# A hybrid encoder layer: a prologue with whole token tiles, and other SBUF places

## The chip, the cores and the metric

The kernel runs on one core of one Trainium2 chip. The metric is the device time of one execution in microseconds; the time before is the median of three runs, 915.5 us (914.26 to 915.56). All inputs lie in the chip's memory at the start, and the output is written there.

## The reference, cut to what matters

One layer of a hybrid trunk, on 512 tokens of width 1024, in float32:

```
h  = rms_norm(x, gain)                        # per token: x * rsqrt(mean(x^2)) * gain
xa, ga, q, k, v, f, gA, gB = split(h @ w_in)  # one projection, 1024 -> 7696 columns
A  = gelu(ga) * rg_lru(causal_conv4(xa))      # recurrent branch, width 1280
B  = forgetting_attention(q, k, v, f)         # 16 heads of 64, causal
m  = sigmoid(gA) * (A @ P_A) + sigmoid(gB) * (B @ P_B)
x  = x + rms_norm(m @ w_out, gain)
h  = rms_norm(x, gain)
u  = causal_conv3(h @ w_up)                   # 1024 -> 6144
x  = x + rms_norm((gelu(u_gate) * u_val) @ w_down, gain)
```

The change concerns how the first normalisation is fed, where some weights lie in SBUF while gA, gB and w_up are multiplied, and when one block of P_B is made ready.

## The kernel before, in words

**Numbers in two parts.** Every operand of a large product is split into a high part, rounded to the format float32r (fp32r in the rows), and a low part, the rest. A product is then three products of parts: high by high, high by low, low by high (mm3, L216; project_half, L226). ScalarE makes the high part (Split.hi, L171, a copy), and VectorE, or GpSimd where lo(pool) is written, the low one (Split.lo, L174, a subtraction). In the rows wh and wl are the parts of weights, hh and hl those of the normalised input (channels on the partitions, tokens along the row, 8 blocks of 128 channels), h2h and h2l those of the second normalised input.

**Stages.** The weights come in units of 128x1024 in the order of the list `order` (L186). fetch (L201) issues a unit's load on the SP queue and its two splits; unit (L210) runs ahead by one or two units. TensorE goes through: four tiles of xa in the prologue (`half`, L623), the other xa, v, ga, the projection P_A, then q0 and k0; the merge gates (`period`, L443); attention over eight pairs of heads with q, k of the next pair (L1072 on); P_B (pb_part, L1056); w_out; w_up (`period` again, after first products at L1244 to L1290); w_down.

**The order of work.** A planner of the framework orders the instructions of each engine, but for the stretches in manual_schedule (L563, L913, L1283, L1352), where they stand as written. `tc.issue_after(i)` keeps the instructions of its block behind i on i's engine. Each engine works its own list in order.

**The prologue (L557 to L691).** GpSimd builds an identity matrix. ScalarE's queue loads one row of gains (`gone`), which TensorE spreads over 128 partitions by a product with a row of ones into two banks (pgain, L588). SP loads token tiles 0 and 1 in two halves of 512 columns each (L570), then the units xa0 and xa1, tiles 2 and 3, xa2 and xa3. For a tile, `sumsq` (L594) squares and sums each half on ScalarE, VectorE adds the two sums, and rstd_of gives the factor (a square root on ScalarE, a reciprocal on VectorE); `sumsq_whole` (L603, tiles 2 and 3) does it in one instruction of 1024 columns. `scaled(t, g)` multiplies half g by the factor and the gains on VectorE, `turn(t, g)` transposes its four blocks on TensorE, and evac_hi and evac_lo write them to hh (ScalarE) and hl (VectorE). `spin(n)` is n products of the identity with itself into a bank that is used later; they compute nothing. The written order is at L626 to L669: tile 0's first half, tile 1's sums, the rounding of unit xa0, then halves of both tiles in turns, then `half(0, X)`: unit xa0 by the first 256 tokens, that is, tiles 0 and 1.

**Gates and up loop.** Both take pairs of output blocks by seven products instead of eight (class Pair, L339). The products are numbered: 1 and 2 multiply plain weights (mh0, ml0, from the pool called stpools[0]) by a quarter of the input; 3 multiplies mh1, ml1 (stpools[1]) by a sum of quarters; 5, 6 and 7 multiply sums of weights (th, tl, in the pool of all weights) by sums of quarters (sh, sl); 4 multiplies th, tl by a plain quarter. In the gates the names carry a g in front: gmh, gml, gth, gtl, gsh, gsl. A pair's stretch runs 5, 6, 4 of the pair before, 3, then 1 and 2 of the next and 7. Each product is 12 products of 256 columns on TensorE (L418, L419, L421).

**Places.** Pools are stacked from the left and the right side of SBUF. `offset(stack, n)` puts n unused bytes (per partition) between two pools. In the kernel before, hh starts at byte 69120, gmh0 at 180160 and 184256 (two buffers), the weights' buffers for gth at multiples of 4096 from 35328, gsh0 at 196544; in the up loop h2h starts at 196544, mh0 at 126464 and 130560, up0's first weights at 85504.

**P_B.** pb_part(e, ks) takes unit pb`e` and, running one ahead, issues the load and splits of the next. pb0, pb1 and pb2 are multiplied in the attention's tail, pb3 to pb7 after it (L1129 to L1131).

Of the kernel before, what the change touches and what calls it, by code (L numbers as in the profile page):

```python
# [8 lines left out]
F32 = mybir.dt.float32  # L9
F32R = mybir.dt.float32r  # L10
BF16 = mybir.dt.bfloat16
AF = mybir.ActivationFunctionType
# [4 lines left out]
P = 128  # L17
# [46 lines left out]
def kernel(  # L64
# [421 lines left out]
    with ExitStack() as rg:  # L486
        rt, ixt, tt = {}, {}, {}
        last_act = [None]
        with ExitStack() as r0:
# [68 lines left out]
            with tc.tile_pool(name="pre", bufs=2, side="right", reuse_waits="tile") as pre, ExitStack() as wp:  # L558
# [3 lines left out]
                man = ExitStack()  # L562
                man.enter_context(tc.manual_schedule())  # L563
                warm = small.tile([P, 1], F32, name="warm", bufs=1)
                gone = pre.tile([1, D + P], F32, name="gone", bufs=1)
                pool.memset(gone[:, D:], 1.0)
                act.dma_start(gone[:, :D], gains[0:1, :])
                act.activation(out=warm, in_=epst, func=AF.Sqrt)
                xts = [pre.tile([P, D], F32, tag="xt", name=f"xt{t}", bufs=NT) for t in range(NT)]
                for t in range(2):  # L570
                    for c in HALVES:
                        nc.sync.dma_start(xts[t][:, c], xv[:, t, c])
                us = [Split(*order[t][1:], order[t][0], wpre) for t in range(2)]
                for t in range(2, NT):
                    nc.sync.dma_start(xts[t], xv[:, t])
# [10 lines left out]

                spin(4)
                pgain = [bank(f"gain{i}") for i in range(2)]  # L588
                for i in range(2):
                    pe.matmul(pgain[i], gone[:, D:], gone[:, 512 * i : 512 * i + 512], start=True, stop=True)  # L590

                xns, rss, ptr, lasts = {}, {}, {}, [None, None]

                def sumsq(t):  # L594
                    xns[t] = pre.tile([P, D], F32, tag="xn", name=f"xn{t}")
                    s2 = small.tile([P, 2], F32, tag="s2", name=f"s2_p{t}")
                    for i, c in enumerate(HALVES):
                        act.activation(out=xns[t][:, c], in_=xts[t][:, c], func=AF.Square, accum_out=s2[:, i : i + 1])
                    ss = small.tile([P, 1], F32, tag="ss", name=f"ss_p{t}")
                    dve.tensor_tensor(out=ss, in0=s2[:, 0:1], in1=s2[:, 1:2], op=ALU.add)  # L600
                    rss[t] = rstd_of(ss, f"p{t}")

                def sumsq_whole(t):  # L603
                    xns[t] = pre.tile([P, D], F32, tag="xn", name=f"xn{t}")
# [18 lines left out]
                def half(i, c):  # L623
                    project_half(pss[i], us[i].parts(), hh, hl, c)

                sumsq(0)  # L626
                scaled(0, 0)
                sumsq(1)
                us[0].hi()
                us[0].lo(pool)  # L630
                scaled(1, 0)
                turn(0, 0)
                spin(3)
                turn(1, 0)
                scaled(0, 1)
                turn(0, 1)
                evac_hi(0, 0)
                evac_lo(0, 0)
                scaled(1, 1)
                turn(1, 1)  # L640
                evac_hi(1, 0)
                evac_lo(1, 0)
                evac_hi(0, 1)
                evac_lo(0, 1)
                evac_hi(1, 1)
                evac_lo(1, 1)
                half(0, X)
                us[1].hi()
                us[1].lo(pool)
                sumsq_whole(2)  # L650
# [256 lines left out]
    with ExitStack() as g2:  # L907
        spool = g2.enter_context(tc.tile_pool(name="gsums", bufs=1, side="right", reuse_waits="tile"))
        gates.sh = [spool.tile([P, KH, SH], F32R, name=f"gsh{i}") for i in range(4)]
        gates.sl = [spool.tile([P, KH, SH], F32R, name=f"gsl{i}") for i in range(4)]  # L910
        gp[1] = Pair(gates, 1, GP[1])
        man = g2.enter_context(ExitStack())
        man.enter_context(tc.manual_schedule())  # L913
        for i, f in enumerate((fq[3], fq[0], fq[2], fq[1])):
            act.copy(gates.sh[i], f)
            sub(gates.sl[i], f, gates.sh[i].bitcast(F32))
        hfstk.close()
        st0pool = splitstk.enter_context(tc.tile_pool(name="gsplit0", bufs=2, side="right", reuse_waits="tile"))
        offset(splitstk, 448, "right")
        st1pool = splitstk.enter_context(tc.tile_pool(name="gsplit1", bufs=2, side="right", reuse_waits="tile"))  # L920
        gates.stpools = [st0pool, st1pool]
        none = Nothing()
        p, n = gp[0], gp[1]
        p.plain_high(0)
        p.plain_high(1)
        p.p12()
        p.p5()
        n.sums(0)
        n.sums(1)
        n.plain_low(0)  # L930
        n.plain_high(0)
        n.sums_hi(0)
        n.sums_hi(1)
        p.keep(2, p.a[:, Y])
        p.add(p.a[:, X], p.a[:, X], 2)
        p.keep(1, p.c[:, X])
        n.sums_lo(0)
        n.sums_lo(1)
        gp[2] = Pair(gates, 2, GP[2])

        def more(j):
            if j + 3 < len(GP):
# [12 lines left out]
        bias = prep_alloc(0)  # L955
        b = gp.pop(len(GP) - 1)
        b.add(b.c[:, Y], b.a[:, Y], 1)
        b.add(b.c[:, X], b.c[:, X], 0)
        gate_epilogue(b, "c", 0)
        fetch(where["k1"])  # L960
        gate_epilogue(b, "c", 1)

    with ExitStack() as at:
# [47 lines left out]
        def pt(p, pts):  # L1011
# [10 lines left out]
            for j in range(2):  # L1022
# [4 lines left out]
                for i0, i1, src, o in ((0, 8, tbs[j], 0), (8, 10, rest, P * j)):  # L1027
                    for half in range(2):
                        ps = src[half][:, o : o + (i1 - i0) * HD].rearrange("p (i c) -> p i c", c=HD)
                        act.copy(thv[:, i0:i1, half], ps)  # L1030
                        dve.tensor_tensor(out=tlv[:, i0:i1, half], in0=ps, in1=thv[:, i0:i1, half].bitcast(F32), op=ALU.subtract)
                res.append((th, tl))
            return res
# [22 lines left out]
        def pb_part(e, ks):  # L1056
            if e not in pb:
                pb[e] = bank(f"pb{e}")
                pbw[e] = unit(f"pb{e}", 1)
            wh, wl = pbw[e]  # L1060
            for k in ks:
                mm3(pb[e], wh[:, k], wl[:, k], yb[k][:, 0], yb[k][:, 1], k == 0, k == KD - 1)

        rounded = []

        def behind(name, ahead=2):
            with tc.issue_after(rounded[-1].ins):
# [70 lines left out]
    mstk.close()  # L1138

    fstk = ctx.enter_context(ExitStack())  # L1140
    offset(fstk, 96)
    xpool = fstk.enter_context(tc.tile_pool(name="x2", bufs=1, reuse_waits="tile"))
    x2t = xpool.tile([P, NT, D], F32, name="x2t")
    nc.sync.dma_start(x2t, xv)
# [14 lines left out]

    turned = {}  # L1160
    with ExitStack() as mix:
        wfpool = mix.enter_context(tc.tile_pool(name="wfirst", bufs=2, reuse_waits="tile"))
        npool = mix.enter_context(tc.tile_pool(name="norm", bufs=2, reuse_waits="tile"))
        special["up0"] = special[f"up{JF}"] = wfpool
        hf = npool.tile([P, KD, S], F32, name="hf", bufs=1)
        gb = [npool.tile([P, D], F32, name=f"gain{i}", bufs=1) for i in range(2)]
        nstk = ExitStack()
# [115 lines left out]
        with tc.manual_schedule():  # L1283
# [8 lines left out]
            p.sums_lo(0)  # L1292
            next(s3, None)

    ypool = fstk.enter_context(tc.tile_pool(name="ff", bufs=3, reuse_waits="tile"))
    ydram = ctx.enter_context(tc.tile_pool(name="ffd", bufs=1, space=bass.MemoryType.DRAM))
    yd = [ydram.tile([P, 2, S], F32, name=f"yd{j}") for j in range(JF // 2)]
# [427 lines left out]
```

## Time and profile before

| | us |
|---|---|
| median of three runs | 915.5 |
| lowest and highest | 914.26, 915.56 |
| the profiled execution | 915.62 |
| its span, from first to last instruction | 913.8 |

The profile is that of one execution. PE is TensorE's products, PEld its weight loads, DVE VectorE, ACT ScalarE, POOL GpSimd, and SPq the SP queue's issue of transfers. A row of the timeline has the start, the length, the engine, the line, the operation, out<-in by names, the shape and the count, and in brackets the idle time before it with what ended it. Products overlap in the pipeline, so a product's own length is longer than its distance to the next; where many follow each other, the time of a whole stretch divided by their count is the pace. A row of a stretch (start:end) has the length, then the busy time of each engine with its count of instructions, the clock, and the load of the DMA engines. A row of a group has the count, and behind the bar the busy time and the mean length in ns.

### The profile page before, as it was taken

The numbers are of one execution on the slowest core, as the hardware profiler recorded it, in microseconds if no ns is written. First come the engines' busy times: TensorE is split into PE (matmuls) and PEld (weight loads), VectorE is DVE, ScalarE is ACT, GpSimd is POOL, SyncE is SP. The second block draws the span as 40 slices with busy tenths as digits, with TensorE's granted clock in tenths as the row PEclk, the third lists the DMA queues.
The fourth block names the chain that finished last, engine by engine and source line by source line (L and its number), as shares of the span: only waits on it lengthen the run. The fifth ranks groups of instructions, "written<-read, shape, count | busy, mean of one in ns | idle before, by whom it ended". The sixth has DMA issues, their size and how long they took to land.

```text
span 913.8 us, 15945 instructions
## 1 busy us (share of the span) xinstructions
PE 904.4 (99%) x5906; PEld 805.5 (88%) x5906; DVE 726.0 (79%) x1197; ACT 601.6 (66%) x1041; POOL 218.9 (24%) x281
## 2 busy tenths in 40 slices
PE   8999999999999999999999999999999999999997
PEld 7988888887899998888888889999999999988886
DVE  4966359737777649888878588989999999889897
ACT  6565496423377757677654477878888888677664
POOL 4134444534111112212104200132323223100000
PEclk9999999999999999999999999999999999999999
DMA  7677669989968767435424654468988888699764
GB/s 261 234 214 207 191 166 274 256 229 182 212 164 198 199 222 261 180 128 174 139 93 156 208 180 160 116 174 201 231 227 209 236 210 211 205 397 328 243 200 148
DMA packets 72048, 187.86 MB, mean 206 GB/s; under 512 B 7265, under 2 KB 27793, under 8 KB 71586
## 3 DMA queue, kind: packets, MB, share of 16 engines
q1 hardware_dynamic: 47648, 127.72, 41.9%
q0 software_dynamic: 24176, 58.99, 29.8%
q8 instruction: 46, 0.75, 0.3%
q14 instruction: 32, 0.26, 0.1%
q10 hardware_dynamic: 146, 0.14, 0.0%
HBM read 150.69 MB, written 35.73 MB: 204 GB/s over the span
## 4 chain that ended last, share of the span: by engine, by line
PE 96%; DVE 1%; DMA 1%; ACT 1%; SPq 0%; issue 0%; DVEq 0%; ACTq 0%
PE up L421 7%; PE up L419 7%; PE up L418 7%; PE dn L1434 4%; PE dn L1432 4%; PE dn L1433 4%; PE pa L217 2%; PE ga L218 2%; PE ga L217 2%; PE pa L219 2%; PE pa L218 2%; PE ga L219 2%; PE k L217 2%; PE q L217 2%; PE wo L1151 2%; PE pb L217 2%
## 5 line engine op out<-in xcount | busy, mean ns | idle before, releaser
L1309 DVE SCALAR_TENSOR_TENSOR u<-up,cpt,u 128x511 f32<-128x511 f32 x96 | 71.3, 746 | 3.5 <-ACT u L1303 1.8
L362 POOL DMA_DIRECT2D ml<-raw_up x41 | 35.3, 861 | 152.6 <-ACT ml L361 89.5
L1434 PE MATMUL dn<-wh_dn,al 128*128 128x512 f32 (+1 forms) x180 | 67.7, 376 | 0.0
L1433 PE MATMUL dn<-wl_dn,ah 128*128 128x512 f32 (+1 forms) x180 | 67.5, 375 | 0.0
L1432 PE MATMUL dn<-wh_dn,ah 128*128 128x512 f32 (+1 forms) x180 | 67.5, 375 | 0.0
L419 PE MATMUL up<-sl,th 128*128 128x256 f32 x252 | 60.2, 276 | 0.0
L418 PE MATMUL up<-sh,th 128*128 128x256 f32 x252 | 60.2, 276 | 0.0
L175 DVE TENSOR_TENSOR wl_dn<-raw_dn,wh_dn 128x1024 fp32r<-128x1024 f32 x42 | 51.3, 1222 | 9.3 <-ACT wh_dn L172 9.2
L172 ACT CAST wh_dn<-raw_dn 128x1024 fp32r<-128x1024 f32 x42 | 44.1, 1050 | 21.2 <-PE dn L1434 7.3
L1303 ACT ACTIVATE u<-up,cpt 128x512 f32<-128x512 f32 x48 | 36.9, 778 | 21.6 <-PE up L421 11.6
L324 DVE TENSOR_TENSOR tl<-t,th 128x1024 fp32r<-128x1024 f32 x42 | 51.0, 1217 | 0.0
L419 PEld LDWEIGHTS up<-sl,th 128*128 128x128 f32 x252 | 47.3, 188 | 0.0
L418 PEld LDWEIGHTS up<-sh,th 128*128 128x128 f32 x252 | 47.3, 188 | 0.0
L1317 POOL TENSOR_TENSOR yf<-u,u 128x512 f32<-128x512 f32 x23 | 31.4, 1365 | 63.3 <-issue 48.8
L400 ACT CAST th<-t 128x1024 fp32r<-128x1024 f32 x42 | 43.8, 1045 | 3.3 <-DVE t L324 0.8
L418 PE MATMUL up<-h2h,mh 128*128 128x256 f32 x168 | 40.2, 276 | 0.0
L419 PE MATMUL up<-h2l,mh 128*128 128x256 f32 x168 | 40.2, 276 | 0.0
L1434 PEld LDWEIGHTS dn<-wh_dn,al 128*128 128x128 f32 x180 | 33.9, 188 | 6.8 <-DVE al L324 0.7
L1433 PEld LDWEIGHTS dn<-wl_dn,ah 128*128 128x128 f32 x180 | 33.9, 188 | 6.1
L1432 PEld LDWEIGHTS dn<-wh_dn,ah 128*128 128x128 f32 x180 | 33.9, 188 | 6.0
L421 PE MATMUL up<-sh,tl 128*128 128x256 f32 x252 | 38.8, 276 | 0.0
L998 ACT ACTIVATE P<-P,mx 128x384 f32<-128x384 f32 (+3 forms) x64 | 35.2, 553 | 4.2 <-DVE mx L993 3.3
(717 smaller groups left out, 3239.1 us busy)
## 6 DMA issues: line engine op xcount, KB each, us to landing
raw_up<-in_w_up_dram SPq DMA_DIRECT2D x48, 512.0 KB, 5.4
td<-in_w_down_dram POOLq DMA_DIRECT2D x36, 512.0 KB, 6.0
raw_dn<-td SPq DMA_DIRECT2D x24, 512.0 KB, 5.2
B<-cnd POOLq DMA_DIRECT2D x16, 640.0 KB, 5.5
ml<-raw_up POOLq DMA_DIRECT2D x20, 512.0 KB, 5.8
raw_dn<-in_w_down_dram SPq DMA_DIRECT2D x18, 512.0 KB, 4.3
raw_wo<-in_w_out_dram SPq DMA_DIRECT2D x16, 512.0 KB, 3.9
td<-td POOLq DMA_DIRECT2D x12, 512.0 KB, 10.6
```

The costliest lines, as they stand in the source:

```text
L172: act.copy(self.wh, self.raw)
L175: engine.tensor_tensor(out=self.wl, in0=self.raw, in1=self.wh.bitcast(F32), op=ALU.subtract)
L217: pe.matmul(dst, ah, bh, start=first, stop=False)
L324: dve.tensor_tensor(out=out, in0=a, in1=b, op=ALU.subtract)
L400: act.copy(self.th[i], self.t[i])
L418: pe.matmul(dst, wh[:, k], ah[:, k], start=first and k == 0, stop=False, skip_group_check=True)
L419: pe.matmul(dst, wh[:, k], al[:, k], start=False, stop=False, skip_group_check=True)
L421: pe.matmul(dst, wl[:, k], ah[:, k], start=False, stop=k == KH - 1, skip_group_check=True)
L1309: dve.scalar_tensor_tensor(out=c[:, s:], in0=ps[:, : S - s], scalar=col(C_CFW + 3 * e + j), in1=c[:, s:], op0=ALU.mult, op1=ALU.add)
L1432: pe.matmul(d[:, x], ah[:, k, tok], wh[:, k, x], start=first, stop=False, skip_group_check=True)
L1433: pe.matmul(d[:, x], ah[:, k, tok], wl[:, k, x], start=False, stop=False, skip_group_check=True)
L1434: pe.matmul(d[:, x], al[:, k, tok], wh[:, k, x], start=False, stop=last, skip_group_check=True)
```

## The change

- Tiles 0 and 1 are loaded by one transfer each, and squared whole (`sumsq_whole`); `sumsq` goes.
- The gains' row is split into a high and a low part on VectorE (four instructions of one partition and 512 columns), and four products of float32r replace the two of float32. The row of ones and the parts lie in buffers of the pool xc; the tile `gone` is 512 bytes shorter.
- Two fillers are added ahead of tile 0's transposes.
- The order of the prologue: both halves of tile 0 are scaled and transposed, then the three fillers, then tile 1's sums, the rounding of unit xa0, tile 0's two high parts; tile 1 is scaled and transposed by halves; the low parts come behind.
- The first stretch of xa0 takes all eight products high by high, then the eight with hl, then the eight with wl, where it took high by high and high by low in turns.
- The 448 bytes between the gates' two weight pools become 384 ahead of the first and 64 between them: the first (gmh0, gml0) moves by 384 bytes, the second stays.
- The 96 bytes ahead of the residual x2t go behind it; the pool of the first up weights is parted in two with 96 bytes between, so that up0's weights move by 96 bytes and up24's stay. What comes later keeps its place.
- In attention's tail the unit fetched ahead by pb_part(2), which is pb3, is held behind the last copy of pair 6's transposed probabilities on ScalarE.

```
-                gone = pre.tile([1, D + P], F32, name="gone", bufs=1)
-                pool.memset(gone[:, D:], 1.0)
-                act.dma_start(gone[:, :D], gains[0:1, :])
+                gone = pre.tile([1, D], F32, name="gone", bufs=1)
+                act.dma_start(gone, gains[0:1, :])
...
                 for t in range(2):
-                    for c in HALVES:
-                        nc.sync.dma_start(xts[t][:, c], xv[:, t, c])
+                    nc.sync.dma_start(xts[t], xv[:, t])
...
-                for i in range(2):
-                    pe.matmul(pgain[i], gone[:, D:], gone[:, 512 * i : 512 * i + 512], start=True, stop=True)
+                one = xpool.tile([P, S], F32R, tag="xc", name="one")[0:1, :P]
+                pool.memset(one.bitcast(F32), 1.0)
+                for i, c in enumerate(HALVES):
+                    gh, gl = (xpool.tile([P, S], F32R, tag=x, name=f"gain_{x}{i}")[0:1] for x in ("xh", "xl"))
+                    dve.tensor_copy(out=gh, in_=gone[:, c])
+                    dve.tensor_tensor(out=gl, in0=gone[:, c], in1=gh.bitcast(F32), op=ALU.subtract)
+                    for j, g in enumerate((gh, gl)):
+                        pe.matmul(pgain[i], one, g, start=j == 0, stop=j == 1)
...
-                sumsq(0)
+                spin(2)
+                sumsq_whole(0)
                 scaled(0, 0)
-                sumsq(1)
+                scaled(0, 1)
+                turn(0, 0)
+                turn(0, 1)
+                spin(3)
+                sumsq_whole(1)
                 us[0].hi()
                 us[0].lo(pool)
-                scaled(1, 0)
-                turn(0, 0)
-                spin(3)
-                turn(1, 0)
-                scaled(0, 1)
-                turn(0, 1)
                 evac_hi(0, 0)
-                evac_lo(0, 0)
-                scaled(1, 1)
-                turn(1, 1)
-                evac_hi(1, 0)
-                evac_lo(1, 0)
                 evac_hi(0, 1)
-                evac_lo(0, 1)
-                evac_hi(1, 1)
-                evac_lo(1, 1)
-                half(0, X)
+                for g in range(2):
+                    scaled(1, g)
+                    turn(1, g)
+                for g in range(2):
+                    evac_lo(0, g)
+                for g in range(2):
+                    evac_hi(1, g)
+                    evac_lo(1, g)
+                wh, wl = us[0].parts()
+                for w, h in ((wh, hh), (wh, hl), (wl, hh)):
+                    for k in range(KD):
+                        pe.matmul(pss[0][:, X], w[:, k], h[:, k, X], start=w is wh and h is hh and k == 0, stop=w is wl and k == KD - 1)
...
+        offset(splitstk, 384, "right")
         st0pool = splitstk.enter_context(tc.tile_pool(name="gsplit0", bufs=2, side="right", reuse_waits="tile"))
-        offset(splitstk, 448, "right")
+        offset(splitstk, 64, "right")
...
-                        act.copy(thv[:, i0:i1, half], ps)
+                        copied[p] = act.copy(thv[:, i0:i1, half], ps)
...
-                pbw[e] = unit(f"pb{e}", 1)
+                with ExitStack() as held_back:
+                    if e == 2:
+                        held_back.enter_context(tc.issue_after(copied[KD - 2].ins))
+                    pbw[e] = unit(f"pb{e}", 1)
...
-    offset(fstk, 96)
     xpool = fstk.enter_context(tc.tile_pool(name="x2", bufs=1, reuse_waits="tile"))
...
-        wfpool = mix.enter_context(tc.tile_pool(name="wfirst", bufs=2, reuse_waits="tile"))
+        wfpools = [mix.enter_context(tc.tile_pool(name="wfirst0", bufs=1, reuse_waits="tile"))]
+        offset(mix, 96)
+        wfpools.append(mix.enter_context(tc.tile_pool(name="wfirst1", bufs=1, reuse_waits="tile")))
...
-        special["up0"] = special[f"up{JF}"] = wfpool
+        special["up0"], special[f"up{JF}"] = wfpools
...
+    offset(fstk, 96)
     ypool = fstk.enter_context(tc.tile_pool(name="ff", bufs=3, reuse_waits="tile"))
```

More of the change, by code (lines that the diff above doesn't have):

```diff
@@ L588 @@
                 pgain = [bank(f"gain{i}") for i in range(2)]
-                for i in range(2):
-                    pe.matmul(pgain[i], gone[:, D:], gone[:, 512 * i : 512 * i + 512], start=True, stop=True)
-                xns, rss, ptr, lasts = {}, {}, {}, [None, None]
[L594 to L601, printed above, removed]
+                one = xpool.tile([P, S], F32R, tag="xc", name="one")[0:1, :P]
[6 more added lines that the diff above has]
+                        pe.matmul(pgain[i], one, g, start=j == 0, stop=j == 1)
+                xns, rss, ptr, lasts = {}, {}, {}, [None, None]
                 def sumsq_whole(t):
@@ L1062, in pb_part @@
                 mm3(pb[e], wh[:, k], wl[:, k], yb[k][:, 0], yb[k][:, 1], k == 0, k == KD - 1)
-        rounded = []
+        rounded, copied = [], {}
         def behind(name, ahead=2):
```

## The prediction

> **What bounds the kernel now.** The first page of the profile comes first, for the span, the load of each engine and the chain that ended last.
>
> ```profile
> span 913.8 us, 15945 instructions
> PE 904.4 (99%) x5906; PEld 805.5 (88%) x5906; DVE 726.0 (79%) x1197; ACT 601.6 (66%) x1041; POOL 218.9 (24%) x281
> PE 96%; DVE 1%; DMA 1%; ACT 1%; SPq 0%; issue 0%; DVEq 0%; ACTq 0%
> ```
>
> TensorE works 99% of the span, and 96% of the chain is TensorE. So I asked the view of waits what TensorE waited for in the whole span, and it has two rows:
>
> ```profile
> PE xa L585 <- POOL ident masks.py:199: 1.5, 1, 1.5
> PE tr_p L245 <- DVE xn L611: 1.2, 1, 1.2
> ```
>
> Both lie in the first 11 us. So three things can shorten this kernel: an earlier start of the products (now 13.65), an earlier end of TensorE's slow pace, and a shorter time per product in the 900 us behind. The timeline of the front:
>
> ```profile
> 0.74 2.19 SPq L572 DMA_DIRECT2D xt<-in_x_dram  x4
> 1.49 2.08 PE L585 MATMUL xa<-ident 128*128 128x128 f32 x8 [1.49 <-POOL ident masks.py:199]
> 2.98 0.91 SPq L166 DMA_DIRECT2D raw_xa<-in_w_in_dram  x2
> 3.50 3.78 PE L590 MATMUL gain<-gone 1*128 1x512 f32 x4
> 3.84 0.63 ACT L598 ACTIVATE xn<-xt 128x512 f32<-128x512 f32 x1 [1.03 <-DMA xt<-in_x_dram]
> 4.47 0.63 ACT L598 ACTIVATE xn<-xt 128x512 f32<-128x512 f32 x1
> 6.02 0.75 DVE L611 SCALAR_TENSOR_TENSOR xn<-xt,rs_p,gain 128x512 f32<-128x512 f32 x1
> 7.21 1.12 PE L245 MATMUL tr_p<-ident,xn 128*128 128x128 f32 x4
> 8.11 1.49 PE L585 MATMUL xa<-ident 128*128 128x128 f32 x6
> 8.54 0.63 ACT L598 ACTIVATE xn<-xt 128x512 f32<-128x512 f32 x1 [2.21 <-DMA xt<-in_x_dram]
> 9.92 1.04 ACT L172 CAST wh_xa<-raw_xa 128x1024 fp32r<-128x1024 f32 x1
> 10.82 3.18 PE L245 MATMUL tr_p<-ident,xn 128*128 128x128 f32 x12 [1.22 <-DVE xn L611]
> 10.87 0.58 ACT L249 CAST hh<-tr_p 128x512 fp32r<-128x512 f32 x1
> 13.65 0.56 PE L229 MATMUL xa<-hh,wh_xa 128*128 128x256 f32 x1
> 15.65 2.42 POOL L175 TENSOR_TENSOR wl_xa<-raw_xa,wh_xa 128x1024 fp32r<-128x1024 f32 x1 [2.20 <-ACT wh_xa L172]
> 16.14 0.41 PE L230 MATMUL xa<-hl,wh_xa 128*128 128x256 f32 x1
> 16.35 0.41 PE L229 MATMUL xa<-hh,wh_xa 128*128 128x256 f32 x1
> 16.78 0.29 PE L229 MATMUL xa<-hh,wh_xa 128*128 128x256 f32 x1
> ```
>
> and, from the chain in order of time (start, length, what):
>
> ```profile
> 20.02 0.94 PE xa L232 x8
> ```
>
> The reader is to see four things. Tile 1's second half lands at 8.54. The first weights land at 9.9, and their rounding on ScalarE holds up tile 0's evacuation, which was ready. VectorE's last scaling stands behind an evacuation, so the last transposes come late. And the first products are 0.21 us apart (16.14 to 16.35), later ones 0.12 (eight in 0.94): TensorE runs at about half pace until 16.7.
>
> **The front.** (1) Issue: SP spends 2.19 us on four half tiles, and 0.91 on two transfers of a whole 512 KB. Two whole tiles cost about 0.9, so all behind them is issued 1.3 us sooner, and the first weights land at about 9.9 - 1.3 = 8.6.
>
> (2) Tile 0 lands between 3.84 (its first half) and 4.47, where ScalarE took the second half; I take 4.3. A whole tile's way to its scaling is shown by tile 2:
>
> ```profile
> 15.46 1.06 ACT L606 ACTIVATE xn<-xt 128x1024 f32<-128x1024 f32 x1
> 17.17 1.41 DVE L611 SCALAR_TENSOR_TENSOR xn<-xt,rs_p,gain 128x512 f32<-128x512 f32 x2
> ```
>
> That is 1.71 us to the start and 3.12 to the end of both halves. Tile 0 is scaled from 6.0 to 7.4, its first half no later than now (6.02). The add of two half sums goes.
>
> (3) The gain rows: two full fp32 products took four passes of 0.94 us (3.78). Four rounded ones replace them. A rounded product of 256 columns takes 0.21 at half pace, so one of 512 about 0.42: 1.7 us. They need two copies and two subtractions of 1x512 on VectorE, at most 0.7 each by the 0.75 of the 128x512 scaling: 2.8 us from 3.5 at worst, done at 6.3 beside tile 0's squaring. Covered; without the cover scaling would start 0.3 late. The two fillers (a third of 1.49 each, 1.0 together) run while tile 0 is scaled.
>
> (4) TensorE then has tile 0's eight transposes (four take 0.9, from 7.21 to 8.11), three fillers (1.4) and tile 1's eight, all in its own order: 6.75 + 1.8 + 1.4 = 9.95, and + 1.8 = 11.7. Tile 1 must be scaled by then. Its landing is not shown for a whole tile. The rate by half-microseconds gives the early bound:
>
> ```profile
> GB/s 0 0 0 41 291 340 365 250 201 254 176 303 369 336 369 381 389 418 393 401 401 451 426 393 418 410 409 400 392 398 338 360 384 168 86 49 25 8 123 131
> ```
>
> Summed, 1.05 MB (both tiles) are in by 5.8; the late bound is today's 8.54. I take 7.0: scaled from 8.7 to 10.1, in time for 9.95 and 10.8. ScalarE rounds the weights from 8.6 to 9.7 and evacuates tile 0 by 10.7, before tile 1 needs it. The lower halves on VectorE run beside the first eight products, which no longer need them: the new order takes all eight upper by upper products first. So the first product starts at about 11.7 instead of 13.65: **1.95 us**. Bounds: with the landing at 8.54 the scaling ends at 11.66, + 0.9 is 12.6, and with the clock opening no earlier half of the 1.05 us is lost: 0.6. At best, below.
>
> (5) The clock. The page's clock line shows no step in the front, so I go by the distance of products. From 1.49 to 9.6 TensorE was hardly idle, with fillers, gain rows and transposes, and stayed at half pace; it sped up 3.05 us after real products began. I take the same distance again, so the start's 1.95 us is kept whole. Were the opening fixed at 16.7, the extra time would be worth 0.12/0.21 of it: 1.1. Were it opened by the denser fillers before 11.7, the 3.05 us at half pace (worth 1.3) would go too, and transposes would shorten: up to 3.9.
>
> [...]
>
> What follows is fed in time: POOL's low part of the second weights ends at 18.07 and is first used at 20.02, the eight products above; its cause, ScalarE's rounding behind the last evacuation, moves forward with the evacuation.
>
> **SBUF places.** They move no work, yet products of one shape differ by operands:
>
> ```profile
> L418 PE MATMUL mb<-gsh,gth 128*128 128x256 f32 x48 | 11.8, 281 | 0.0
> L418 PE MATMUL mb<-hh,gmh 128*128 128x256 f32 x32 | 7.7, 276 | 0.0
> L418 PE MATMUL mb<-hh,gth 128*128 128x256 f32 x16 | 4.0, 282 | 0.0
> L418 PE MATMUL up<-sh,th 128*128 128x256 f32 x252 | 60.2, 276 | 0.0
> 280.63:284.87 4.24, 4.24 (x39) 4.24 (x37) 3.02 (x7) 2.86 (x6) 0.86 (x1) 1.00 0.97 280
> 600.47:604.54 4.07, 4.07 (x38) 4.07 (x37) 2.61 (x5) 3.15 (x7) 2.67 (x3) 1.00 0.17 65
> ```
>
> The last two are 36 products each (7, 5 and 6) of a gates pair and of an up pair: 4.24 against 4.07 us. By the allocator's addresses in the kernel before, the moving tile's place less the weights', modulo 512, is 448 in both; but in the gates the products ahead (hh by gmh) stand at 64, while in the up loop they stand at 448 as well. So the pace seems to be lost at the switch from 64 to 448. The 384 bytes put gmh0 and gml0 at 448 from hh, like the rest. If the pace then holds, 0.17 us times eight pairs is 1.4; I keep **1.1 us**, since the first pair or two enter from another state than the rest. Bounds: nothing, 1.4, or, if hh by gmh went to the 282 of hh by gth, 192 x 6 ns = 1.2 us lost. I take the row of the up loop, whose places are the same.
>
> The up loop's first products show the same two paces, 48 products each:
>
> ```profile
> 555.70:561.35 5.65, 5.65 (x49) 5.65 (x48) 5.65 (x11) 3.69 (x10) 0.00 (x0) 1.00 0.72 220
> 579.83:585.26 5.43, 5.43 (x50) 5.43 (x49) 5.40 (x8) 5.26 (x8) 0.87 (x1) 1.00 0.56 180
> ```
>
> The 96 bytes now stand between up0's weights and up24's; up0's move alone. That can end the slow pace after up0: 0.3 us at most, and up0's second half may slow by 0.1. I take **0.2**. The residual's move touches no product.
>
> **The held-back unit.** The last fetch before the tail puts pb3's rounding here:
>
> ```profile
> 453.51 1.05 ACT L172 CAST wh_pb<-raw_pb 128x1024 fp32r<-128x1024 f32 x1 [2.47 <-PE k L218]
> 454.47 0.57 ACT L970 CAST h_k<-k 128x512 fp32r<-128x512 f32 x1
> 455.74 0.68 DVE L971 TENSOR_TENSOR l_k<-k,h_k 128x512 fp32r<-128x512 f32 x1
> 467.09 0.46 ACT L1030 CAST PTh<-pt_r 128x128 fp32r<-128x128 f32 x2 [1.31 <-DVE PTl L1031]
> 469.25 0.58 ACT L1048 COPY ytmp<-av 64x512 f32<-64x512 f32 x1 [1.70 <-PE av L1045]
> ```
>
> It stands ahead of k7's upper half, which the last scores need. The new wait puts it behind the copies that end at 467.55; ScalarE has 1.70 us free there, and 1.05 fit. Queued behind it on ScalarE is the copy ytmp, for which VectorE's sum y and then the last unit's attention output wait; the copy loses nothing as long as the 1.70 hold. VectorE's low part follows the rounding, and pb3 is multiplied only behind the whole tail (L1131). The gain is at most the 1.05 by which k7's half came late, and the view of waits has no row of TensorE for it, so it is near nothing: **0.1**. The loss is at most 1.05, if the copy waited for the whole rounding.
>
> **Sum.** 1.95 + 1.1 + 0.2 + 0.1 = 3.35 us. The profiled execution took 915.62 us (span 913.8 and 1.8 around it), 0.1 above the median of 915.5. 915.62 - 3.35 = **912.3 us**.
>
> **The rivals.** *The clock opens at the same moment*: for it, the 8 us at half pace; against it, nothing fixes 16.7. The front gives 1.1: 913.1. [...] *The fillers open it early*: for it, TensorE is unbroken from 6.75; against it, the same 8 us. The front gives 1.95 + 1.0 (half to all of the 1.3): 911.3. *Tile 1 lands where it does now and the places do nothing*: for it, the 2.21 us wait for a half of tile 1, and no run shows gmh at its new place. Only the 0.6 of the front stays: 915.0, no change. *Slower*: the up loop falls into the slow pace as the gates have it. A pair's 36 products would cost 0.17 us more, and by the same 5 ns its 24 of products 1 and 2 0.12; the 252 of the row above, 12 a pair, make 21 pairs: 21 x 0.29 = 6.1, and 915.62 - 3.35 + 6.1 = 918.4. It passes the time before from the twelfth slow pair on. For it: its first 96 products are slow today, and the places there change; against it: today the last tile's transposes, among those first products, end that.
>
> **How the numbers follow.** 0.40 for the forecast, 0.22 for the same moment, 0.15 for the early clock, 0.14 for no change, 0.09 for slower. The range 910.2 to 915.3 reaches from the early clock with its upper bound to the case without change; it leaves out the slow up loop and a little at the fast end. A difference of 0.2% (1.8 us) is about what a measurement of this kernel can tell from none: under 913.8 is faster. The first three cases are faster but for a few parts in a hundred: 0.76; the same 0.15; slower 0.09.
>
> **What would show it.** Right: the first L229-like product near 11.7, the distance of products falling to 0.12 near 14.8 (11.7 + 3.05), the gates' gsh by gth at 276, wh_pb behind 467. Wrong: tile 1's squaring starting at 8.5, gsh by gth still at 281, or up products at 281.

## The result, and the profile after

| | before | changed | ratio, 95% interval |
|---|---|---|---|
| median of 22 runs each | 914.54 us (913.03 to 916.43) | 913.12 us (912.10 to 914.45) | 0.9983 (0.9977 to 0.9989) |
| profiled execution | 915.62 us, span 913.8 | 912.16 us, span 910.4 | |

By the medians the change gains 1.4 us (1.0 to 2.1 by the interval), 0.17%: under the prediction's bound of 0.2%, so "the same" by that bound, though the interval excludes zero. The two profiled executions differ by 3.5 us. That overstates it: the profile of before lies 1.1 above its median, the profile of after at the fast end of its kernel. A comparison of just these two traces would have confirmed the forecast of 3.35.

The page of after, for the span and the load:

```profile
span 910.4 us, 15950 instructions
PE 901.1 (99%) x5910; PEld 804.1 (88%) x5910; DVE 727.8 (80%) x1199; ACT 601.6 (66%) x1037; POOL 220.2 (24%) x281
```

The timeline of its front (start, length, what, idle before it):

```profile
0.75 0.87 SPq L570 DMA_DIRECT2D xt<-in_x_dram  x2
4.51 1.06 ACT L601 ACTIVATE xn<-xt 128x1024 f32<-128x1024 f32 x1 [1.70 <-DMA xt<-in_x_dram]
4.95 0.62 PE L594 MATMUL gain<-gain_xl,one 1*128 1x512 f32 x1
5.50 1.22 PE L583 MATMUL xa<-ident 128*128 128x128 f32 x4
7.18 1.94 PE L245 MATMUL tr_p<-ident,xn 128*128 128x128 f32 x8 [0.46 <-DVE xn L606]
7.25 1.03 ACT L172 CAST wh_xa<-raw_xa 128x1024 fp32r<-128x1024 f32 x1
8.91 0.89 PE L583 MATMUL xa<-ident 128*128 128x128 f32 x6
9.64 1.04 PE L245 MATMUL tr_p<-ident,xn 128*128 128x128 f32 x8
10.91 1.23 PE L644 MATMUL xa<-hh,wh_xa 128*128 128x256 f32 x8 [0.24 <-ACT hh L249]
11.98 1.10 PE L644 MATMUL xa<-hl,wh_xa 128*128 128x256 f32 x8
```

Look at the two rows of fillers: four passes take 1.22 us at 5.50, six take 0.89 at 8.91. Tile 0's eight transposes take 1.94, tile 1's 1.04. TensorE came to full pace at about 9, before the first product. The trace's record of the granted clock, which the views do not print, has it open at 9.03, against 16.79 in the profile of before. The first product starts at 10.91 instead of 13.65, and the first half unit ends 4.1 us earlier.

In the gates, the groups of products of their stretch (count, busy us, mean ns of one, idle before), and in a second fence the held-back rounding from ScalarE's timeline:

```profile
L418 PE MATMUL ma<-gsh,gth 128*128 128x256 f32 x48 | 11.6, 278 | 0.0
L418 PE MATMUL mb<-gsh,gth 128*128 128x256 f32 x48 | 11.5, 277 | 0.0
L418 PE MATMUL mb<-hh,gmh 128*128 128x256 f32 x32 | 7.9, 281 | 0.0
L421 PE MATMUL mb<-hh,gml 128*128 128x256 f32 x32 | 5.1, 281 | 0.0
```

```profile
463.52 1.05 ACT L172 CAST wh_pb<-raw_pb 128x1024 fp32r<-128x1024 f32 x1
```

The 281 of gsh by gth went to 277 (276 was predicted). But hh by gmh, 276 before, now takes the 281: the slow pace has moved to another product. The rounding stands at 463.5; with the 3.84 us by which all of that stage is earlier this is 467.4 in the time of before, where the prediction looked for it.

The waits of TensorE in the whole span:

```profile
PE xa L583 <- POOL ident masks.py:199: 1.5, 1, 1.5
PE tr_p L245 <- DVE xn L606: 0.5, 1, 0.5
PE tr_f L260 <- DVE xn L1197: 0.4, 1, 0.4
PE xa L644 <- ACT hh L249: 0.2, 1, 0.2
```

The third is new and lies at 561 us: part of the gain is given back there, ahead of the last norm's transposes.

### The profile page after: what moved, and what is told of

Same layout as the page of the kernel before. It is cut to its first block, busy times and chain, and to the rows that moved or that the text cites. A ratio compares the mean times of both kernels' runs of the same rounds, so it can differ in the third digit from the quotient of the medians.

```text
span 910.4 us, 15950 instructions
## 1 busy us (share of the span) xinstructions
PE 901.1 (99%) x5910; PEld 804.1 (88%) x5910; DVE 727.8 (80%) x1199; ACT 601.6 (66%) x1037; POOL 220.2 (24%) x281
## 4 chain that ended last, share of the span: by engine, by line
PE 97%; DVE 1%; ACT 1%; DMA 0%; issue 0%; DVEq 0%; ACTq 0%
PE up L421 7%; PE up L418 7%; PE up L419 7%; PE dn L1437 4%; PE dn L1435 4%; PE dn L1436 4%; PE pa L217 2%; PE ga L218 2%; PE ga L217 2%; PE pa L219 2%; PE pa L218 2%; PE ga L219 2%; PE k L217 2%; PE q L217 2%; PE q L219 2%; PE k L218 2%
## 5 line engine op out<-in xcount | busy, mean ns | idle before, releaser
L1306 ACT ACTIVATE u<-up,cpt 128x512 f32<-128x512 f32 x48 | 36.9, 778 | 21.8 <-PE up L421 11.8
```

## The experiments

The theory after the comparison: the front carries the gain, its size hangs on when the clock opens (when TensorE goes from half to full pace; in the profile of before, products of 256 columns from 0.21 us apart to 0.12), and the places mostly move a slow pace about. All kernels ran five rounds; the table gives each median, its own kernel before, and the ratio. Intervals are about 0.9 us to either side (1.4 for e10, which had one execution at 919.46), so 0.5 us between two rows is nothing by itself. Each kernel has one profile.

| kernel | median us (runs) | before | ratio, 95% |
|---|---|---|---|
| e1_front | 913.29 (11) | 914.56 | 0.9986 (0.9976 to 0.9996) |
| e2_places | 913.92 (11) | 914.56 | 0.9992 (0.9983 to 1.0000) |
| e3_two_fewer | 913.25 (11) | 914.56 | 0.9985 (0.9976 to 0.9994) |
| e4_unbroken | 911.82 (5) | 914.56 | 0.9966 (0.9954 to 0.9979) |
| e5_wide_rows | 911.61 (8) | 914.75 | 0.9969 (0.9958 to 0.9981) |
| e6_third_filler | 912.73 (11) | 914.75 | 0.9981 (0.9971 to 0.9990) |
| e7_one_place | 914.89 (12) | 914.75 | 1.0004 (0.9994 to 1.0014) |
| e8_half_tiles | 912.78 (11) | 914.75 | 0.9980 (0.9970 to 0.9991) |
| e9_before_wide | 914.68 (11) | 914.62 | 0.9995 (0.9987 to 1.0004) |
| e10_up_place | 911.51 (12) | 914.62 | 0.9971 (0.9955 to 0.9986) |
| e11_old_gain_rows | 914.96 (11) | 914.62 | 0.9998 (0.9989 to 1.0006) |
| e12_old_order | 913.93 (11) | 914.62 | 0.9990 (0.9981 to 0.9999) |

### The two halves of the change

**e1_front**: the diff's lines of the prologue on the kernel before.

> The kernel before with the front's edits alone (whole tiles 0 and 1, rounded gain rows, two fillers, weights' rounding ahead, new order of the first products); no SBUF place and no held-back unit. Theory A, the front carries the measured gain of 1.4 us: 1.1 to 1.5 us under the kernel before, so level with the changed kernel within 0.3; gsh by gth stays at 281 ns and hh by gmh at 276. Rival B, the front is worth little because the clock opens at a moment of its own, and the places bring the gain: under 0.6 us below the kernel before. Theory A also says that the clock's opening, read from the distance of the first products, lies anywhere from 9 to 13 us in a single profile.

It gained 1.27 us: theory A's number, and B is too low. The gates keep their 76.8 us.

**e2_places**: the other lines of the diff on the kernel before.

> The kernel before with the rest alone: the SBUF places of the gates' and the up loop's operands and the held-back unit; the front is that of before. Theory A: 0 to 0.3 us under the kernel before; gates' gsh by gth at 276 to 278 but hh by gmh at 280 to 281, so that a pair gains about as much as it loses. Rival B: 1.0 us or more below the kernel before, with both products at 276.

It gained 0.64, between the two. By the intervals alone 1.27 and 0.64 can't be told apart; that the front carries most rests on the stages below and on e11. The groups of its gates did what theory A said:

```profile
L418 PE MATMUL ma<-gsh,gth 128*128 128x256 f32 x48 | 11.6, 277 | 0.0
L418 PE MATMUL mb<-hh,gmh 128*128 128x256 f32 x32 | 7.9, 281 | 0.0
```

The start times of stages show the sizes. From the start of ma0 to that of q1 the gates take 76.78 or 76.79 us in the three kernels with the old places (before, e1, e9). With the new ones they take 76.37 in seven profiles of ten, 76.52, 76.59 and 76.64 in e10, e3 and after (e7, with other places again, stands apart). From q1 to the second block of the last head pair's scores it is 119.14 with the old order of pb3's rounding and 119.00 to 119.04 with the new. The first unit of the up loop takes 5.65 before and 5.53 with the moved place, in each profile. So the places and the hold are worth 0.15 to 0.4, 0.1 and 0.1.

### What opens the clock

**e3_two_fewer** leaves out the added fillers, **e6_third_filler** adds one to them:

```
-                spin(2)
                 sumsq_whole(0)
```

```
-                spin(2)
+                spin(3)
                 sumsq_whole(0)
```

> The changed kernel without the two added fillers, so that TensorE idles from the gain rows' end (5.6 us) to tile 0's transposes (7.2). If dense work ahead of the first product opens the clock (theory C): the clock opens later than 9.0 in most executions, 0.4 to 1.0 us slower than the changed kernel. If fillers and transposes do not count (rival D, the early opening in the one profile was chance): the same within 0.2 us.

> The changed kernel with a third added filler alone; the gain rows stay on one partition. Theory C1 (wide rows count): 913.0 to 913.4, no better than the changed kernel, the clock opening between 9 and 12.4 us. Theory C2 (the break counts): 911.7 to 912.2, opening before 9 us.

913.25 and 912.73, against 913.12: no difference from the change that can be told. Theory C's loss of 0.4 to 1.0 did not show in e3, and e6 lies between the ranges of C1 and C2. The number of fillers made no difference that these runs can show.

**e4_unbroken** and **e5_wide_rows**: the gain rows are multiplied over 128 partitions; e4 has a third filler as well.

```
-                one = xpool.tile([P, S], F32R, tag="xc", name="one")[0:1, :P]
+                one = xpool.tile([P, S], F32R, tag="xc", name="one")[:, :P]
...
+                wide = [[xpool.tile([P, S], F32R, tag=x, name=f"gain_{x}{i}") for x in ("xh", "xl")] for i in range(2)]
+                for ws in wide:
+                    for g in ws:
+                        dve.memset(g.bitcast(F32), 0.0)
...
-                    gh, gl = (xpool.tile([P, S], F32R, tag=x, name=f"gain_{x}{i}")[0:1] for x in ("xh", "xl"))
+                    gh, gl = (g[0:1] for g in wide[i])
...
-                    for j, g in enumerate((gh, gl)):
+                    for j, g in enumerate(wide[i]):
```

> The changed kernel with no break in the front: three added fillers instead of two, and the gain rows multiplied over all 128 partitions (127 of them zeros) instead of one, so that the array is busy in every row from 1.5 us on. [...] Rival D, fillers do not count: 913.1 with the spread of 2.3 us as now.

> The changed kernel with the gain rows alone multiplied over 128 partitions (two added fillers, as in the change). The kernel with wide rows and a third filler took 911.82 us against 913.12 of the changed one. [...] Theory C2, the third filler closes the break ahead of tile 0's transposes and that is what counts: 913.1, as the changed kernel.

911.82 and 911.61: 1.3 and 1.5 us under the changed kernel. The zeros add nothing to the sums, TensorE gets no work less, and the third filler makes no difference here either. C2's 913.1 did not come in e5, nor rival D's 913.1 in e4; e5, with the wide rows alone, speaks for C1. The spread is 2.1 us in e4, near the 2.3 of the changed kernel, and 1.1 in e5. TensorE's timeline in the front of e5:

```profile
4.36 0.80 PE L598 MATMUL gain<-gain_xl,one 128*128 128x512 f32 x1
4.95 0.58 PE L598 MATMUL gain<-gain_xh,one 128*128 128x512 f32 x1
5.41 0.50 PE L598 MATMUL gain<-gain_xl,one 128*128 128x512 f32 x1
5.75 0.61 PE L583 MATMUL xa<-ident 128*128 128x128 f32 x4
7.17 1.22 PE L245 MATMUL tr_p<-ident,xn 128*128 128x128 f32 x8 [0.82 <-ACT xn L605]
10.79 1.24 PE L648 MATMUL xa<-hh,wh_xa 128*128 128x256 f32 x8 [0.85 <-ACT hh L249]
```

The last gain row takes 0.50, and four filler passes take 0.61, not 1.22: full pace from about 5.3 on, nearly 4 us before the profile of after. Yet the first product comes only 0.1 us earlier than in after (10.79, not 10.91), since TensorE now waits 0.85 for ScalarE's evacuation, and the two profiled executions take about the same, 912.33 and 912.16. So here an opening at 5.3 bought little more than one at 9. The first product of the four profiles with wide rows in this front comes at 10.44 to 10.98, never as late as the 11.6 to 11.9 of e6, e3 and e12; whether that is what the wide rows buy, single profiles can't show. Such an early opening is not the rule either: by the clock record the four profiles with wide rows in this front open at 5.35, 8.12, 8.39 (e7) and 8.96 (e10), the six with narrow rounded ones at 9.03 (after), 9.15 (e8), 9.38 (e1), 10.57 (e6), 12.00 (e12) and 12.71 (e3). Both kinds scatter. All of the first lie before all of the second, but the closest two, 8.96 and 9.03, hardly differ. C1 is carried by the medians of e4, e5 and e10 (911.51 to 911.82), each under every other kernel's; how the wide rows bring the time is not shown.

The counterpart is **e11_old_gain_rows**, the changed kernel with the two fp32 rows of before on one partition (their ones are set in `gone` again):

```
-                one = xpool.tile([P, S], F32R, tag="xc", name="one")[0:1, :P]
...
-                        pe.matmul(pgain[i], one, g, start=j == 0, stop=j == 1)
+                for i in range(2):
+                    pe.matmul(pgain[i], gone[:, D:], gone[:, 512 * i : 512 * i + 512], start=True, stop=True)
```

> The changed kernel with the gain rows of before: two fp32 products on one partition, four passes of 0.94 us. By the prediction's step 3 they end at 7.3 instead of 5.6 us; the two fillers then end at 8.4, tile 0's transposes at 10.1, tile 1's at 12: first product 12.2 to 12.8 and 0.7 to 1.3 us slower than the changed kernel. Rival: the first product hangs on tile 1's landing alone, 10.9 to 11.4 and within 0.3 us of the changed kernel.

914.96, 1.8 us slower than the change and level with before: a little past the expected end, and the largest loss of any step taken back. So rounding the gain rows is what the front of this change cannot do without. Its front:

```profile
3.50 3.78 PE L589 MATMUL gain<-gone 1*128 1x512 f32 x4
7.20 1.22 PE L584 MATMUL xa<-ident 128*128 128x128 f32 x4
8.22 1.91 PE L245 MATMUL tr_p<-ident,xn 128*128 128x128 f32 x8
9.93 1.49 PE L584 MATMUL xa<-ident 128*128 128x128 f32 x6
11.20 1.76 PE L245 MATMUL tr_p<-ident,xn 128*128 128x128 f32 x8
12.94 1.44 PE L639 MATMUL xa<-hh,wh_xa 128*128 128x256 f32 x8
14.22 1.10 PE L639 MATMUL xa<-hl,wh_xa 128*128 128x256 f32 x8
```

TensorE has no break from 1.49 on, and yet the fillers (1.49 for six passes) and nearly all the transposes run at half pace; the clock record opens at 12.67. A busy TensorE was not enough here: it worked 11.2 us, 3.8 of them gain rows on one partition, before the clock opened. In e5, with its rows on 128 partitions, the clock opened 3.9 us after TensorE's start; in e4, e7 and e10 it took 6.6 to 7.5.

**e9_before_wide**: the one edit on the kernel before.

```
-                gone = pre.tile([1, D + P], F32, name="gone", bufs=1)
+                gone = pre.tile([P, D + P], F32, name="gone", bufs=1)
                 pool.memset(gone[:, D:], 1.0)
-                act.dma_start(gone[:, :D], gains[0:1, :])
+                dve.memset(gone[:, :D], 0.0)
+                act.dma_start(gone[0:1, :D], gains[0:1, :])
```

> The kernel before with one edit: its gain rows multiplied over 128 partitions, 127 of them zeros, instead of one. All else, the half tiles, the fp32 gain rows and the order of the first products too, is as before. [...] Rival G, the gain of the change comes from its earlier and reordered work, not from the clock: within 0.4 us of the kernel before.

914.68, no gain: G's number. But the kernel isn't the clean trial that it was meant to be:

```profile
5.60 3.75 PE L591 MATMUL gain<-gone 128*128 128x512 f32 x4 [2.02 <-DMA gone<-in_gains_dram]
10.00 1.24 PE L586 MATMUL xa<-ident 128*128 128x128 f32 x6
11.07 1.04 PE L245 MATMUL tr_p<-ident,xn 128*128 128x128 f32 x8
```

The fetch of the gains had to wait for the zeros to be written, so the rows start 2.1 us late and TensorE idles. Full pace comes at about 11 (10.83 by the clock record), before the first product at 12.98 but far from e5's 5.35, and the front's work is late by as much as the rows. It settles nothing on the time.

### The front's other steps

**e8_half_tiles**: the four half tile fetches again.

```
-                    nc.sync.dma_start(xts[t], xv[:, t])
+                    for c in HALVES:
+                        nc.sync.dma_start(xts[t][:, c], xv[:, t, c])
```

> The changed kernel with tiles 0 and 1 fetched by halves again, all else as changed. By the prediction's step 1, all behind the four transfers is issued later, the first weights' rounding on ScalarE waits for them and holds tile 0's evacuation: first product 0.8 to 1.3 us later than 10.9, and 0.4 to 1.2 us slower than the changed kernel. Rival: the landing is limited by the bandwidth of 1 MB and not by the issue, so weights land as now: within 0.2 us of the changed kernel.

912.78: the rival's number, no loss at all, though the work isn't where it was. On ScalarE the rounding of the first weights is 0.7 us later than in after (7.93, not 7.25), behind tile 1, whose squaring starts at 6.48 and not at 5.89; the first product of its profile starts at 10.80 all the same.

**e12_old_order**: upper and lower halves by turns again.

```
-                wh, wl = us[0].parts()
-                for w, h in ((wh, hh), (wh, hl), (wl, hh)):
...
+                half(0, X)
```

> The changed kernel with the first eight products of the upper halves in their old order, upper and lower by turns. By the prediction's step 4 the second product then waits for the lower halves on VectorE, which come at 11.5 and 12.2 us: TensorE idles 0.5 to 1.3 us there, and the kernel is 0.4 to 1.2 us slower than the changed one. Rival: the lower halves come in time for a TensorE at half pace, so within 0.2 us where the clock opens late.

913.93, 0.8 slower than the change by the medians and 0.6 by the ratios: in the expected range, though the two intervals overlap. Its timeline shows the wait for the lower halves, 0.31 us where 0.5 to 1.3 were expected. Its clock also opened late (12.00), so this one profile can't say how much of the loss is the order's:

```profile
11.90 0.42 PE L229 MATMUL xa<-hh,wh_xa 128*128 128x256 f32 x1
12.63 0.39 PE L230 MATMUL xa<-hl,wh_xa 128*128 128x256 f32 x1 [0.31 <-DVE hl L253]
```

### The places

**e7_one_place**, on e4: hh and hl moved to 448, the gates' weights to 0.

```
-    offset(mstk, 96)
+    offset(mstk, 32)
...
+    offset(mstk, 64)
...
-                offset(wp, 256, "right")
+                offset(wp, 192, "right")
...
-        offset(splitstk, 384, "right")
+        offset(splitstk, 448, "right")
-        offset(splitstk, 64, "right")
```

> The kernel with wide rows and three fillers, and places so chosen that every product of 256 columns in the front and the gates has its moving tile at 448 and its weights at 0 modulo 512, as most products of the up loop have; the changed kernel has hh by gmh at 0 and 64, hh by gth at 0 and 0, gsh by gth at 448 and 0. Theory E, the slow pace comes from a change of the two places between products and not from their difference, which is 448 on both sides of the switch: all gates rows at 272 to 277 ns, the gates' stretch 1.2 to 1.8 us shorter than 76.6, and 910.0 to 910.8 us. Theory F, the pace is a state that a stall or any switch of tiles can flip, whatever the places: one of the large groups still at 280 or more, the stretch within 0.4 of 76.6, and 911.4 to 912.2 us.

914.89, 3.1 slower than e4: both theories miss the time. Yet theory E has the paces of the gates right, as the same groups show:

```profile
L419 PE MATMUL mb<-gsh,gth 128*128 128x256 f32 x48 | 11.5, 276 | 0.0
L419 PE MATMUL mb<-hh,gmh 128*128 128x256 f32 x32 | 7.6, 276 | 0.0
L419 PE MATMUL ma<-hh,gth 128*128 128x256 f32 x16 | 3.8, 276 | 0.0
```

All three at 276: the slow group has gone instead of moving. The stretch is only 0.4 us shorter than in e4 (75.96 us), not 1.2 to 1.8 under 76.6: the faster products save 1.2, and 0.8 of it goes to a pause in the first pair, most of it this wait:

```profile
PE ma L419 <- DVE ma L438: 0.6, 1, 0.6
```

In these rows hh by gmh stands 448 apart as in after, at 281 there; gsh by gth had the very places of e7 in the kernel before and took 281. So in these runs neither the difference nor the place of one product settles its pace. Theory E's estimate, that a change of places between neighbouring products does, fits the 276 of e7 and e10; it is not shown, and the last section has one group at 276 and at 281 in the same places. The time was lost in products that the expectation did not look at, those of 512 columns, here by e7 and then by after:

```profile
L217 PE MATMUL ga<-hh,wh_ga 128*128 128x512 f32 x80 | 31.6, 396 | 0.0
```

```profile
L217 PE MATMUL ga<-hh,wh_ga 128*128 128x512 f32 x80 | 31.1, 389 | 0.0
```

With hh at 0 they are 7 ns shorter than at 448. Some 770 products of 512 columns have hh or hl as the moving tile; their groups are 5 to 7 ns longer in e7 than in e4, some 4.6 us in all, of which the gates give 0.4 back. The two profiles differ by 4.0.

**e10_up_place**, on e5:

```
-        offset(ustk, 32, "right")
+        offset(ustk, 448, "right")
...
-        offset(ustk, 416, "right")
```

> The changed kernel with wide gain rows (911.61 us) and one place more: the weights of the up loop's product 3 go from 416 to 0 modulo 512, so that all products of a pair stand at 448 and 0. Theory E, products of 256 columns that stay at one pair of places 448 apart keep the fast pace: the 252 products of sh by mh fall from about 280 to 276 ns, 0.7 to 0.9 us less, 910.6 to 911.1 us. Rival H, the pace follows the state that the neighbours leave: 911.4 us or more.

911.51 against e5's 911.61: by the medians nothing, rival H's bound. The profile shows theory E's effect, here for e5 and then for e10:

```profile
L418 PE MATMUL up<-sh,mh 128*128 128x256 f32 x69 | 16.9, 279 | 0.0
L421 PE MATMUL up<-sh,ml 128*128 128x256 f32 x72 | 11.3, 278 | 0.0
```

```profile
L418 PE MATMUL up<-sh,mh 128*128 128x256 f32 x72 | 17.2, 276 | 0.0
L421 PE MATMUL up<-sh,ml 128*128 128x256 f32 x72 | 11.1, 276 | 0.0
```

The up loop (up3's start to the first down product) takes 199.60 us in e2 to e6, e8, e11 and e12, 200.01 in after, and 198.75 in e10. In e10's one profile 0.4 us more than in e5 had been lost at tile 2's transposes just before. Whether 0.8 us are there in the time stays open. e5 and e10, 3.1 us under their kernels before, are the fastest of all and beat both kernels.

## Why the prediction was right or wrong

The time 913.12 lies in the range, 0.8 above the forecast; the gain, 1.4 where 3.35 was forecast, is less than half, and the case given most, faster by over 0.2%, did not come. That the time came so close is in part luck: two errors, 1.1 in the base and 1.9 in the gain, offset each other.

- **The base.** The sum was taken from an execution at 915.62, said to stand 0.1 above the median of three runs. With 22 runs it stands 1.1 above. This error hid part of the other one in the time.
- **Step 1, issue: wrong.** 1.3 us of earlier issue were to bring the rest forward. SP did as said (0.87 us), but e8 has the old fetches and loses nothing.
- **Steps 2 and 3: right.** Tile 0 lands near 4.5, its scaling starts at 6.3; the rounded rows end at 5.6. e11 shows how much they carry, 1.4 to 1.8 us by ratio or median. The prediction counted them as one link of a chain.
- **Step 4: right in kind.** The first product came at 10.91 with the clock open, and at 11.6, 11.8 and 11.9 in e6, e3 and e12, where it opened late: 11.7 was a fair price for the late case. The new order's worth, 0.6 to 0.8 by e12, is not clear of the noise.
- **Step 5, the clock: the mechanism failed.** "It sped up 3.05 us after real products began": in after it did so 1.9 us before the first. That execution showed the rival with the early clock, but not each does: in the profile of e12, whose front is the same up to its first products, the clock record opens at 12.0. The rival with the clock at the same moment gives 913.1, the measured time, but for the wrong reason: nothing holds the opening at 16.7. It was read off one profile that happened to open late; e2, with the front of before, opened at 13.54.
- **SBUF places: the step that cost most.** "If the pace then holds", 1.1 us. It held for gsh by gth and was lost for hh by gmh: 0.15 in after, 0.4 in most. The bound "if hh by gmh went to the 282" was on record and came true, beside the gain instead of without it. "The pace seems to be lost at the switch from 64 to 448" is refuted: hh by gmh and the products of gsh on either side of it all stand at 448 now, and it is slow.
- **First up 0.2, hold 0.1: right**, 0.12 and 0.10 to 0.14.
- **What had no term: give-backs.** From the start of q0 to that of k0, ten of eleven profiles with the new front (e11 counted among them) take 5.68 to 6.31 us, the eleventh (e3) 5.50, and the three with the old front (before, e2, e9) 5.46 to 5.49. The view of waits names this one in e11, beside the one at tile 2:

```profile
PE q L219 <- DVE wl_q L175: 0.6, 1, 0.6
PE tr_f L260 <- DVE xn L1192: 0.4, 1, 0.4
```

VectorE's queue stands there behind a fetch of the forget gate's sums, and in e11 it starts after it 12.3 us ahead of q0, in before 13.3. Why the fetch is later against TensorE no run settled. The wait at tile 2 is not seen with the front alone (e1) or the places alone (e2); it is in after and in seven of the nine kernels made from it, but in e9 too, so the halves together are not its only cause. It fits that the halves, 1.27 and 0.64, add to more than the whole 1.42; the intervals alone would allow that as well.

The price of the slow up loop, 6.1 us, was not paid: in after sh by th takes 276 as in before, and sh by mh 280.

## What to carry to other kernels

Before explaining 0.3%, find out how far executions of the kernel before differ among themselves and at which event: one profile of each kernel here told 3.5 us where 1.4 were to be had. Whether TensorE was busy did not tell when its clock opened: in e11 it had no break from 1.49 us on, and the clock opened at 12.67. One row of real data padded with zeros to 128 partitions brought, on top of the change, as much again as the whole change (911.6 us, against 913.1), by what way is not shown; on the kernel before, where the zeros held up the fetch of the row, it brought nothing (914.7). A place in SBUF is to be judged by all products that read the tile. In the change, 384 bytes took gsh by gth from 281 to 277 ns and hh by gmh from 276 to 281; in e7, the places that put hh by gmh and gsh by gth at 276 took ga's products with hh from 389 to 396, and the kernel was 3.1 us slower than e4.

## What the runs showed of the hardware

**When the clock opened.** By the clock record TensorE has its full clock from 16.79 us in before, 13.54 in e2 and 10.83 in e9, and in the profiles with the new front from anywhere between 5.35 (e5) and 12.71 (e3). It stays so for 894.29 us (before, e2), 897.71 (after and most others), 901.12 (e5) or 904.53 (e7); no run shows what sets these lengths. e2 has the front of before and opened 3.25 us earlier, so the same moment, which one rival of the prediction took for granted, did not hold even with one front. In after TensorE had, behind its gain rows, four filler passes (1.22 us from 5.50), 0.46 of idling and eight transposes (1.94 from 7.18) before the clock opened at 9.03, and no product of the layer. e12 had the same fillers and transposes without that break (1.22 from 6.14, 1.94 from 7.15), and its clock opened at 12.00. Nor did work without a break settle the moment: with the gain rows on one partition the clock opened at 9.38 in e1, 12.00 in e12 and 12.67 in e11, with the rows on 128 partitions at 8.12 in e4, and in e5, with 0.82 of idling after its opening, at 5.35. What opens it, these runs don't tell.

**Two paces of one product.** Products of 256 columns ran 113 or 118 ns apart here with the same operands in the same places. In the up loop's first units, second halves, the kernels after and e5 have the same places:

```profile
L229 PE MATMUL up<-h2h,wh_up 128*128 128x256 f32 x37 | 8.6, 276 | 0.0
```

```profile
L229 PE MATMUL up<-h2h,wh_up 128*128 128x256 f32 x36 | 8.7, 281 | 0.0
```

The first is after, the second e5, both between 569 and 581 us. The stretch from tile 3's transposes to up3 takes 22.5 to 22.6 us in six profiles and 23.25 to 23.4 in eight. The two values, 0.65 us apart, occur with the old places (before, e1) and with the new ones (after, e5), so in these runs the places alone did not settle the pace of over a hundred products in a row; what did is not shown. Whether it differs between executions of one kernel is not shown, since each has one profile. The gates' groups shown of e7 and the pairs' of e10 take 276; in both kernels this stretch is slow, its groups at 281 and 282.
